# Adding the seven Strassen products up in PSUM banks, in the projections of a hybrid attention encoder layer

## The chip, the cores and the metric

The kernel runs as one program on one core of a Trainium2 chip. A core has a matrix engine (TensorE, "PE" in the profile, its weight loads "PEld"), a vector engine (VectorE, "DVE"), a scalar engine (ScalarE, "ACT"), a general engine (GpSimd, "POOL") and a queue that issues the transfers (SyncE, "SP"). The metric is the device time of one execution in microseconds; of several runs the median counts.

## What is computed

One encoder layer with d = 1024 over two batches that share the weights: a prompt of 512 tokens and a sample of 1024 tokens, all in float32. Cut to what matters here:

```python
def encoder_layer(x, ...):
    h = rms_norm(x, g_norm)
    u = h @ w_in                      # 1024 x 9728
    qa, ka, va, za, qb, kb, vb, zb, qc, kc, vc, zc, gl = jnp.split(u, offs, axis=-1)
    ya = neighborhood_attention(...)  # mixer A
    yb = diff_attention(...)          # mixer B
    yc = dilated_attention(...)       # mixer C
    pa = (ya * jax.nn.silu(za)) @ w_br_a
    ...
    merged = gates[:, :, 0] * pa + gates[:, :, 1] * pb + gates[:, :, 2] * pc
    return x + merged @ w_out
y = rms_norm(encoder_layer(x_prompt, ...), g_final)   # and the same of x_sample
```

## The kernel before

**Products.** `h @ w_in` and `merged @ w_out` are multiplied by Strassen's scheme in Winograd's form. A step takes two tiles of 128 columns of the weights (a *pair*), both halves of the 1024 rows, and both halves of the tokens: 256 tokens a half in the prompt, 512 in the sample. Instead of eight products of a quarter it makes seven, of sums of the weights (`s1` to `s4`, tiles `ws`) with sums of the tokens (`t1` to `t4`, made once by `sums`). Each product is twelve matmuls into one PSUM bank (`mm3`): the weights' rounded part `wh`, their remainder `wl`, and `wh` or a bfloat16 copy `wb` against the tokens' remainder. So a product needs a cast (`wh`), a subtraction (`wl <- x - wh`) and often a second cast (`wb`) before it, on ScalarE, VectorE or GpSimd. The tokens' operands are the tiles `tp` (prompt, and `tpb`, `tpl` for remainders), `th` and `tl` (sample). `strassen` does this for pairs and, at the end, for the output projection; `strassen_v` does it for three groups of four column tiles whose result is wanted with tokens on the partitions (weights' tiles `wq`).

**Adding up.** The seven products go to PSUM tiles named `p`, of which there are two (`PSUM_TAGS`). The first is copied to an SBUF tile `c`; each of the others is added to or from a `c` by VectorE, seven times in all, with the order that the formulas give: `c00`, then `c01` from `c00`, `c10` from `c01`, `c11` from `c10`. In the output projection the last addition goes to the residual tile `xt` straight from PSUM (`early`).

**Order.** All instructions are recorded first. `Program.order` then plays them through a model of the engines: an instruction that is ready and has a slot for its tiles is taken by the engine that is free, the oldest first, and that order is emitted. A copy or a cast may go to ScalarE or VectorE (`copy`, "AD"), a sum without PSUM to VectorE or GpSimd, and `better` gives it to the engine that the model thinks is done first. The engines of `wl` are fixed by a table (`LE`), those of `ws` are GpSimd (`SE`). The eight PSUM banks are one class `b` with a cap for each tag:

```python
RESERVE = {'e': 2, 's': 0, 'p': 2}
...
PSUM_TAGS = {'p': 2, 's': 3, 't': 2, 'o': 1}
for _t, _n in PSUM_TAGS.items():
    CAPS[_t] = ("b", _n)
```

Here `s` is scores, `t` transposes, `o` attention outputs. Every emitted instruction has the same source line (L418), so rows are told apart by tiles.

**Stages.** The prompt's 38 steps come first. The sample's 38 steps follow, with the attention units of both batches spread between them. Then the branches are merged (`merge`), and the output projection runs in six calls of `output`.

Of the kernel before, what the change touches and what calls it, by code (L numbers as in the profile page):

```python
# [18 lines left out]
D = 1024  # L19
# [49 lines left out]
class Buf:  # L69
    """A logical tile: one of the slots of its tag holds it from its first to its last instruction."""  # L70

    def __init__(self, prog, tag, shape, dtype, name):
        self.prog, self.tag, self.shape, self.dtype, self.name = prog, tag, list(shape), dtype, name
        self.free = int(np.prod(shape[1:]))
        self.seq = self.slot = self.real = None
        self.left = 0
        self.acc, self.last = [], []
# [68 lines left out]
class Program:  # L146
    """Records instructions, orders them by a model of the engines, and emits them in that order."""
# [92 lines left out]
    def price(self, eng, meth, args, kw):  # L240
        """Microseconds that an instruction holds its engine, those to its result, and those of the DMA rings."""
# [179 lines left out]
# the scheduler: latency between engines, instructions looked ahead, slots of a tag that stay free for older tiles  # L421
# [3 lines left out]
# engines of the sums of weights (P: GpSimd, D: VectorE), of the low parts of weights for the seven products of a pair  # L425
# (prompt, sample beside mixer B, sample beside the others), and query tiles whose two maps GpSimd joins in mixer B
# [4 lines left out]
# where the sample's operands are made, pairs multiplied directly, slots of the column quads, and the attention units:  # L431
# their starts in slots of the sample's stream and their order
# [8 lines left out]
# slots of each size, and for each tag its size and how many it may hold  # L441
# [14 lines left out]
PSUM_TAGS = {'p': 2, 's': 3, 't': 2, 'o': 1}  # L456
# [4 lines left out]
def build(ctx, tc, a):  # L461
# [18 lines left out]
    def copy(dst, src, scale=None, engines="AD"):  # L480
        """dst <- scale * src, on the engine that is done first."""
# [12 lines left out]
    def split(hi, lo, x, scale=None, psum=False, lo_on="DP"):  # L494
        """hi <- round(scale * x), lo <- scale * x - hi, both float32r."""
# [19 lines left out]
    def preamble():  # L515
# [15 lines left out]
        # padded relative position bias, masked outside each query column's window  # L531
# [31 lines left out]
    def put(dst, src, t, lo_on="DP"):  # L563
        """Columns 128 t .. of an operand (hi, lo) <- src."""
# [8 lines left out]
    def sums(T, t, f):  # L573
        """The operands of T that are sums, of the quarters in f, which is overwritten."""
# [8 lines left out]
        tt(f10, f11, f10, OP.subtract)  # L583
# [78 lines left out]
    def split_w(raw, lo_on="DP", half=True):  # L662
        """hi and lo of [128, n, 128] weights, and their bfloat16 or once more hi."""
# [10 lines left out]
    def mm3(ps, w, xh, xl):  # L674
        """ps <- the sum of w[k]^T (xh[k] + xl[k]) over k."""
        n = len(xh)
        for k in range(n):
            pe.matmul(ps, w[0][k], xh[k], start=k == 0, stop=False)
        for k in range(n):
            pe.matmul(ps, w[1][k], xh[k], start=False, stop=False)  # L680
        for k in range(n):
            pe.matmul(ps, w[2][k], xl[k], start=False, stop=k == n - 1)

    def strassen(raw, T, n, put, direct=False, early=None):
        """raw^T times the matrix of T: put(i, j, tile) for tile i of the 256 columns of raw and half j of T's."""
# [19 lines left out]
        def mul(x, q, on):  # L705
            hi, lo = T[q]
            w = split_w(x, on, q not in ("t1", "t2", "t3"))
            ps = pg.tile("p", [128, 512], F32)[:, :n]
            mm3(ps, w, [hi[:, k] for k in range(4)],
                [lo[k // 2][:, k % 2] if isinstance(lo, list) else lo[:, k] for k in range(4)])  # L710
# [24 lines left out]
        c01 = out(0, 1)  # L735
# [5 lines left out]
        p = mul(a1, "b10", LX[2])  # L741
        tt(c00, p, c00, OP.add, "D")
        done(0, 0, c00)
        c10 = out(1, 0)
        yield
        p = mul(s3, "t3", LX[3])
        tt(c10, p, c01, OP.add, "D")
        c11 = out(1, 1)
# [6 lines left out]
        p = mul(b1, "t4", LX[5])  # L755
        tt(c10, c10, p, OP.subtract, "D")
        done(1, 0, c10)
        yield
        if early:
            early(0, 1, c01)  # L760
            done(0, 1, mul(s4, "b11", LX[6]))
        else:
            p = mul(s4, "b11", LX[6])
            tt(c01, p, c01, OP.add, "D")
            done(0, 1, c01)
# [817 lines left out]
```

## Time and profile before

| | |
|---|---|
| runs | 2077.75, 2090.3, 2093.19 us, median 2090.3 |
| span of the profiled execution | 2095.2 us |
| TensorE | busy 1957.3 us, 93%, granted clock 0.979 on the mean |
| VectorE | busy 1733.3 us, 83% |
| ScalarE | busy 1053.0 us, 50% |
| GpSimd | busy 1108.8 us, 53% |
| DMA | 287.20 MB, 137 GB/s |

The profile is of one execution, whose span runs from its first to its last instruction; no other time of that execution is shown. Busy is not the same as working: TensorE's matmuls overlap, and an instruction of VectorE or GpSimd that is held up after its start counts as busy.

### The profile page before, as it was taken

The numbers are of one execution on the slowest core, as the hardware profiler recorded it, in microseconds if no ns is written. First come the engines' busy times: TensorE is split into PE (matmuls) and PEld (weight loads), VectorE is DVE, ScalarE is ACT, GpSimd is POOL, SyncE is SP. The second block draws the span as 40 slices with busy tenths as digits, with TensorE's granted clock in tenths as the row PEclk, the third lists the DMA queues.
The fourth block names the chain that finished last, engine by engine and source line by source line (L and its number), as shares of the span: only waits on it lengthen the run. The fifth ranks groups of instructions, "written<-read, shape, count | busy, mean of one in ns | idle before, by whom it ended". The sixth has DMA issues, their size and how long they took to land. (4 is left out here: it accounts for less than half of the span.)

```text
span 2095.2 us, 33259 instructions
## 1 busy us (share of the span) xinstructions
PE 1957.3 (93%) x11436; PEld 1490.6 (71%) x11436; DVE 1733.3 (83%) x3029; ACT 1053.0 (50%) x2052; POOL 1108.8 (53%) x788
## 2 busy tenths in 40 slices
PE   6998988788999999999999999999999999999998
PEld 6988877777877766666766677776765666666675
DVE  8999999999888577787888898566578777999698
ACT  5554455554455453254555546456546656544243
POOL 4897786767445344445454353632554333432485
PEclk9999999999999999999999999998999999999999
DMA  5554433435233435352213132333445455876642
GB/s 170 158 176 137 147 110 117 139 124 170 71 117 101 142 115 183 99 168 75 86 66 102 56 100 101 116 112 119 126 128 169 119 146 176 278 261 224 239 150 91
DMA packets 242343, 287.20 MB, mean 137 GB/s; under 512 B 33182, under 2 KB 168574, under 8 KB 242174
## 3 DMA queue, kind: packets, MB, share of 16 engines
q1 hardware_dynamic: 242174, 285.08, 42.6%
q8 instruction: 90, 1.47, 0.3%
q14 instruction: 79, 0.65, 0.1%
HBM read 203.93 MB, written 81.44 MB: 136 GB/s over the span
## 5 line engine op out<-in xcount | busy, mean ns | idle before, releaser
L418 PE MATMUL p<-th,wh 128*128 128x512 f32 x1400 | 435.4, 424 | 2.6 <-ACT wh L418 2.3
L418 DVE TENSOR_TENSOR c<-p,c 128x512 f32<-128x512 f32 (+1 forms) x462 | 260.2, 576 | 160.4 <-PE p L418 143.3
L418 POOL TENSOR_TENSOR wl<-ws,wh 128x512 fp32r<-128x512 f32 x143 | 202.9, 1419 | 263.7 <-ACT wh L418 133.6
L418 POOL TENSOR_TENSOR wl<-raw,wh 128x512 fp32r<-128x512 f32 (+1 forms) x159 | 228.8, 1439 | 185.2 <-PE o L418 42.5
L418 POOL TENSOR_TENSOR ws<-raw 128x512 f32<-128x512 f32 x156 | 233.2, 1496 | 147.6 <-DMA raw<-w_in 60.3
L418 PEld LDWEIGHTS p<-th,wh 128*128 128x128 f32 x1400 | 251.5, 191 | 75.1 <-issue 21.0
L418 PE MATMUL p<-th,wl 128*128 128x512 f32 x1016 | 297.8, 404 | 0.5 <-DVE wl L418 0.4
L418 ACT ACTIVATE wb<-raw 128x512 bf16<-128x512 f32 (+1 forms) x232 | 141.9, 612 | 235.9 <-PE p L418 134.5
L418 PE MATMUL s<-qk 128*128 128x512 f32 (+5 forms) x736 | 228.7, 422 | 7.3 <-DVE qk L418 5.3
L418 PEld LDWEIGHTS p<-th,wl 128*128 128x128 f32 x1016 | 188.7, 191 | 43.7 <-issue 5.6
L418 PEld LDWEIGHTS <-wb 128*128 128x128 bf16 x1376 | 107.0, 98 | 109.9 <-issue 54.1
L418 PE MATMUL p<-tp,wl 128*128 128x256 f32 x892 | 153.0, 294 | 34.3 <-DVE wl L418 32.7
L418 PEld LDWEIGHTS s<-qk 128*128 128x128 f32 (+1 forms) x736 | 117.0, 190 | 92.3 <-issue 61.3
L418 ACT ACTIVATE pt<-t 128x512 fp32r<-128x512 f32 (+4 forms) x173 | 90.4, 542 | 161.8 <-PE t L418 148.7
L418 PE MATMUL p<-tl,wb 128*128 128x512 bf16 x608 | 167.1, 384 | 0.0
L418 PE MATMUL p<-tp,wh 128*128 128x256 f32 x892 | 156.4, 298 | 8.1 <-DVE wh L418 7.1
L418 PEld LDWEIGHTS p<-tp,wl 128*128 128x128 f32 x892 | 124.0, 194 | 47.7 <-DVE wl L418 45.1
L418 ACT ACTIVATE e<-e,st 128x384 f32<-128x384 f32 (+2 forms) x192 | 105.5, 551 | 103.1 <-DVE st L418 101.8
L418 DVE TENSOR_TENSOR wl<-ws,wh 128x512 fp32r<-128x512 f32 x133 | 152.2, 1146 | 1.5
L418 DVE CUSTOM_DVE_ANT_0 e<-s,tab 128x384 f32<-128x384 f32 (+3 forms) x256 | 129.2, 531 | 28.8 <-PE s L418 23.1
L418 ACT ACTIVATE wh<-raw 128x512 fp32r<-128x512 f32 (+1 forms) x211 | 127.4, 604 | 41.5 <-PE p L418 9.7
L418 PE MATMUL t<-ident,e 128*128 128x128 f32 x672 | 123.6, 281 | 16.0 <-DVE e L418 14.4
(235 smaller groups left out, 4230.3 us busy)
## 6 DMA issues: line engine op xcount, KB each, us to landing
raw<-w_in SPq DMA_DIRECT2D x140, 512.0 KB
Us<-c SPq DMA_DIRECT2D x128, 256.0 KB
Up<-c SPq DMA_DIRECT2D x64, 256.0 KB
stg<-Us SPq DMA_DIRECT2D x30, 512.0 KB
g<-Us SPq DMA_DIRECT2D x48, 256.0 KB
tab<-E SPq DMA_DIRECT2D x192, 48.0 KB
stp<-Up SPq DMA_DIRECT2D x30, 256.0 KB
YG<-y SPq DMA_DIRECT2D x30, 256.0 KB
```

Of the source, the lines that this page charges most:

```text
L418: getattr(engs[o.eng], o.meth)(*[val(x) for x in o.args], **{k: val(x) for k, x in o.kw.items()})
```

## The change

`strassen` and `strassen_v` open one bank `A` with the first product (`a0 b00`), copy it out, add the next product into the same bank, copy that out, and so on. Four results leave that bank as copies: `c00`'s part, `c01`'s part, `c11`'s part and `c10`. Two other banks serve the rest: `B` takes `a1 b10`, which is added to `c00`; `C` takes `s1 t1`, which is added to `c11`, and then `s4 b11` on top of it, which is added to `c01`. To make all signs positive, the sum `t4` of the tokens is taken the other way round. The order of the products is a0 b00, a1 b10, s2 t2, s1 t1, s3 t3, b1 t4, s4 b11. `p` may have four banks instead of two, the caps of the other tags stay. In the output projection `early` takes the two copies `c00` and `c01` to the residual at once, and three results go to it straight from PSUM. `strassen_v` makes four sums of weights instead of five. The engines' tables and the model's prices are the same.

```diff
-PSUM_TAGS = {'p': 2, 's': 3, 't': 2, 'o': 1}
+PSUM_TAGS = {'p': 4, 's': 3, 't': 2, 'o': 1}
...
             if kw["start"]:
                 preds.update(o for p0, p1, o in b.last if p0 < box[1] and box[0] < p1)
+                b.opened = [x for x in b.opened if x[0] >= box[1] or box[0] >= x[1]] + [(box[0], box[1], op)]
+            else:
+                preds.update(o for p0, p1, o in b.opened if p0 < box[1] and box[0] < p1)
...
-        tt(f10, f11, f10, OP.subtract)
+        tt(f10, f10, f11, OP.subtract)
...
-    def mm3(ps, w, xh, xl):
+    def mm3(ps, w, xh, xl, first=True):
...
-            pe.matmul(ps, w[0][k], xh[k], start=k == 0, stop=False)
+            pe.matmul(ps, w[0][k], xh[k], start=first and k == 0, stop=False, **kw)
...
+        def part(i, j, ps):
+
+            c = out(i, j)
+            copy(c, ps)
+            if early and i + j < 2:
+                early(i, j, c)
+            return c
+
+        def rest(i, j, c, ps):
+
+            if early and i + j < 2:
+                done(i, j, ps)
+            else:
+                tt(c, ps, c, OP.add, "D")
+                done(i, j, c)
...
-        c00 = out(0, 0)
-        p = mul(a0, "b00", LX[0])
-        copy(c00, p)
+        A = mul(a0, "b00", LX[0])
+        c00 = part(0, 0, A)
+        yield
+        B = mul(a1, "b10", LX[2])
+        rest(0, 0, c00, B)
...
-        p = mul(s2, "t2", LX[1])
-        tt(c01, p, c00, OP.add, "D")
+        mul(s2, "t2", LX[1], A)
+        c01 = part(0, 1, A)
...
-        p = mul(s1, "t1", LX[4])
-        tt(c11, p, c10, OP.add, "D")
-        done(1, 1, c11)
-        tt(c01, p, c01, OP.add, "D")
+        C = mul(s1, "t1", LX[4])
+        yield
+        mul(s3, "t3", LX[3], A)
+        c11 = part(1, 1, A)
+        rest(1, 1, c11, C)
...
+        mul(b1, "t4", LX[5], A)
...
+            c10 = out(1, 0)
+            copy(c10, A)
+            done(1, 0, c10)
+        yield
+        mul(s4, "b11", LX[6], C)
+        rest(0, 1, c01, C)
```

What it does to the order is seen in one pair of the prompt, the last before the first group of four. First TensorE's queue, in the kernel before. `tp_722`, `tp_734` and `tp_793` are t3, t1 and t4; each product has a bank of its own name (`p_2795`, `p_2812`, `p_2837`):

```order
L418 MATMUL p_2795<-tp_722,wh_2752 128x256 [waits Activation_49]
L418 MATMUL p_2795<-tp_722,wh_2752 128x256 x3
L418 MATMUL p_2795<-tp_722,wl_2766 128x256 [waits DVE_49]
L418 MATMUL p_2795<-tp_722,wl_2766 128x256 x3
L418 MATMUL p_2795<-tpb_760,wh_2752 128x256 x2
L418 MATMUL p_2795<-tpb_766,wh_2752 128x256 x2
L418 MATMUL p_2812<-tp_734,wh_2775 128x256 [waits Activation_49]
L418 MATMUL p_2812<-tp_734,wh_2775 128x256 x3
L418 MATMUL p_2812<-tp_734,wl_2791 128x256 [waits DVE_49]
L418 MATMUL p_2812<-tp_734,wl_2791 128x256 x3
L418 MATMUL p_2812<-tpl_748,wh_2775 128x256 x4
L418 MATMUL p_2837<-tp_793,wh_2785 128x256 [waits Activation_49]
```

The same place of the changed kernel, one pair earlier, where `p_2487` is bank A (`tp_724` is t3, `tp_795` t4), `p_2569` bank C and `p_2635` the next pair's A:

```order
L421 MATMUL p_2569<-tpl_755,wh_2542 128x256 x4
L421 MATMUL p_2487<-tp_724,wh_2564 128x256 [waits Activation_49]
L421 MATMUL p_2487<-tp_724,wh_2564 128x256 x3
L421 MATMUL p_2487<-tp_724,wl_2594 128x256 [waits DVE_49]
L421 MATMUL p_2487<-tp_724,wl_2594 128x256 x3
L421 MATMUL p_2487<-tpb_728,wh_2564 128x256 x2
L421 MATMUL p_2487<-tpb_768,wh_2564 128x256 x2
L421 MATMUL p_2635<-tp_578,wh_2629 128x256 [waits DVE_49]
L421 MATMUL p_2635<-tp_578,wh_2629 128x256
L421 MATMUL p_2487<-tp_795,wh_2603 128x256 [waits Activation_49]
L421 MATMUL p_2487<-tp_795,wh_2603 128x256 x3
```

The products t3 and t4 now stand in one bank with two matmuls of the next pair between them, and the wait for ScalarE at t4's first matmul is for the copy that empties the bank.

Then VectorE's queue, of before:

```order
L418 TENSOR_TENSOR c_2769<-p_2741,c_2769 128x256 [waits PE_49,Activation_49,Pool_49]
L418 TENSOR_TENSOR wl_2791<-ws_2637,wh_2775 128x512 [waits DVE_49,PE_49,Activation_49]
L418 TENSOR_TENSOR c_2769<-p_2773,c_2769 128x256 [waits DVE_49,PE_49]
L418 TENSOR_TENSOR c_2822<-p_2795,c_2769 128x256 [waits DVE_49,PE_49]
L418 CAST wq_2829<-rawq_2458 128x512 [waits DMAHW6_49]
L418 TENSOR_TENSOR wl_2834<-ws_2737,wh_2814 128x512 [waits Activation_49]
L418 TENSOR_TENSOR c_2822<-p_2812,c_2822 128x256 [waits DVE_49,PE_49]
L418 TENSOR_TENSOR c_2769<-p_2812,c_2769 128x256
```

and of the changed kernel:

```order
L421 TENSOR_TENSOR c_2572<-p_2530,c_2572 128x256 [waits PE_49,Activation_49]
L421 TENSOR_TENSOR wl_2594<-ws_2500,wh_2564 128x512
L421 CAST wh_2603<-raw_2240 128x512 [waits DMAHW4_49]
L421 CAST wh_2609<-ws_2539 128x512 [waits PE_49]
L421 TENSOR_TENSOR wl_2622<-ws_2539,wh_2609 128x512 [waits DVE_49,PE_49]
L421 CAST wh_2629<-raw_2328 128x512 [waits DMAHW2_49,PE_49]
L421 TENSOR_TENSOR c_2633<-p_2569,c_2633 128x256 [waits DMAHW6_49,Activation_49]
L421 CAST wh_2644<-raw_2387 128x512 [waits PE_49]
L421 TENSOR_TENSOR wl_2669<-raw_2387,wh_2644 128x512 [waits DVE_49,PE_49,Pool_49]
L421 TENSOR_TENSOR c_2572<-p_2569,c_2572 128x256 [waits PE_49]
```

Fewer additions out of PSUM stand there, and the casts `wh` that ScalarE did have moved in between. Counted over the whole order, VectorE has 318 additions out of PSUM fewer, 150 casts `wh` and 45 copies out of `p` more (3029 instructions become 2961); ScalarE has 183 copies out of `p` more and 150 casts `wh` fewer (1727 become 1717); GpSimd has 18 fewer (788 become 770). The matmuls and the transfers are the same in number.

## Rows read from the trace of the kernel before

**Rows 1.** The page: busy time, share and instructions of an engine.

```profile
PE 1957.3 (93%) x11436; PEld 1490.6 (71%) x11436; DVE 1733.3 (83%) x3029; ACT 1053.0 (50%) x2052; POOL 1108.8 (53%) x788
```

**Rows 2.** Busy time by stage: stretch, length; PE, PEld, DVE, ACT, POOL; clock, DMA.

```profile
0.00:530.00 530.00, 456.29 (x3511) 420.25 (x3512) 497.64 (x679) 275.20 (x508) 389.07 (x265) 0.98 0.46 145
530.00:1750.00 1220.00, 1171.90 (x6425) 846.07 (x6424) 937.64 (x1910) 632.73 (x1233) 558.26 (x401) 0.98 0.36 114
1960.00:2095.20 135.20, 125.64 (x550) 90.32 (x548) 114.12 (x137) 51.92 (x113) 97.65 (x72) 0.98 0.40 147
```

**Rows 3.** Waits of PE, 0 to 530 us: us in total, times, longest.

```profile
PE p L418 <- DVE wl L418: 32.7, 42, 1.9
PE p L418 <- DVE wq L418: 16.3, 18, 2.1
PE t L418 <- DVE xp L418: 14.9, 4, 8.4
PE p L418 <- DVE wh L418: 7.1, 8, 2.2
```

**Rows 4.** Waits of PE, 530 to 1800 us, first and fifth.

```profile
PE t L418 <- DVE e L418: 14.4, 15, 2.3
...
PE o L418 <- DVE pt L418: 5.1, 4, 3.8
```

**Rows 5.** Timeline of VectorE, 299.9 to 309.2 us: start, length, instruction.

```profile
300.40 1.50 DVE L418 CAST wq<-ws 128x512 fp32r<-128x512 f32 x1
...
304.13 1.76 DVE L418 TENSOR_TENSOR wq<-ws,wq 128x512 fp32r<-128x512 f32 x1
...
308.22 0.68 DVE L418 TENSOR_TENSOR wq<-ws,wq 128x512 fp32r<-128x512 f32 x1
308.82 0.41 DVE L418 CAST wq<-rawq 128x512 fp32r<-128x512 f32 x1
```

**Rows 6.** Timeline of GpSimd in that stretch, and one instruction at 2081 us.

```profile
299.89 3.16 POOL L418 TENSOR_TENSOR ws<-rawq 128x512 f32<-128x512 f32 x2
303.83 1.50 POOL L418 TENSOR_TENSOR wl<-raw,wh 128x512 fp32r<-128x512 f32 x1 [0.78 <-ACT wq L418]
...
2081.38 1.28 POOL L418 TENSOR_TENSOR wl<-ws,wh 128x512 fp32r<-128x512 f32 x1 [3.24 <-ACT wh L418]
```

**Rows 7.** Groups of VectorE, 0 to 530 us: count, busy us, mean ns, idle before.

```profile
L418 DVE TENSOR_TENSOR c<-p,c 128x256 f32<-128x256 f32 x186 | 73.6, 413 | 10.6 <-PE p L418 10.3
L418 DVE CAST wh<-ws 128x512 fp32r<-128x512 f32 x39 | 38.8, 994 | 2.1 <-POOL ws L418 2.0
...
L418 DVE CAST wh<-raw 128x512 fp32r<-128x512 f32 x5 | 4.1, 822 | 0.0
```

**Rows 8.** Groups of VectorE and ScalarE, whole span.

```profile
L418 DVE TENSOR_TENSOR c<-p,c 128x512 f32<-128x512 f32 x276 | 186.6, 686 | 149.9 <-PE p L418 133.0 <-issue 6.3 <-ACT ft L418 3.7
L418 DVE CAST wh<-ws 128x512 fp32r<-128x512 f32 x82 | 65.4, 798 | 2.1 <-POOL ws L418 2.0
L418 DVE CAST wh<-raw 128x512 fp32r<-128x512 f32 x47 | 34.6, 737 | 0.0
...
L418 ACT ACTIVATE c<-p 128x512 f32<-128x512 f32 x39 | 22.9, 587 | 21.4 <-PE p L418 20.5 <-ACT qk L418 0.8
...
L418 ACT ACTIVATE c<-p 128x256 f32<-128x256 f32 x34 | 12.7, 374 | 7.3 <-PE p L418 5.7 <-POOL ws L418 1.6
```

**Rows 9.** Timeline around one copy out of PSUM, 61 to 85 us.

```profile
60.94 0.61 PE L418 MATMUL p<-tpb,wb 128*128 128x256 bf16 x4
...
61.65 0.39 ACT L418 ACTIVATE c<-p 128x256 f32<-128x256 f32 x1 [0.83 <-PE p L418]
...
82.09 1.66 DVE L418 TENSOR_TENSOR wl<-ws,wh 128x512 fp32r<-128x512 f32 x1
...
83.80 0.74 PE L418 MATMUL p<-tp,wl 128*128 128x256 f32 x4
```

**Rows 10.** Waits of all engines: who waited for whom, us in total, times, longest.

```profile
ACT e L418 <- DVE st L418: 101.8, 67, 8.2
```

More of the change, by code (lines that the diff above doesn't have):

```diff
@@ L76, in __init__ @@
         self.left = 0
-        self.acc, self.last = [], []
+        self.acc, self.last, self.opened = [], [], []
 class View:
@@ L672, in split_w @@
         return [[w[:, k] for k in range(n)] for w in ws]
[L674 removed]
+    def mm3(ps, w, xh, xl, first=True):
         n = len(xh)
+        kw = {} if first else {"skip_group_check": True}
         for k in range(n):
[L678 removed]
+            pe.matmul(ps, w[0][k], xh[k], start=first and k == 0, stop=False, **kw)
         for k in range(n):
[L680 removed]
+            pe.matmul(ps, w[1][k], xh[k], start=False, stop=False, **kw)
         for k in range(n):
[L682 removed]
+            pe.matmul(ps, w[2][k], xl[k], start=False, stop=k == n - 1, **kw)
     def strassen(raw, T, n, put, direct=False, early=None):
@@ L703, in ws, with mul @@
             return s
-        def mul(x, q, on):
+        def mul(x, q, on, ps=None):
             hi, lo = T[q]
             w = split_w(x, on, q not in ("t1", "t2", "t3"))
-            ps = pg.tile("p", [128, 512], F32)[:, :n]
+            first = ps is None
+            if first:
+                ps = pg.tile("p", [128, 512], F32)[:, :n]
             mm3(ps, w, [hi[:, k] for k in range(4)],
-                [lo[k // 2][:, k % 2] if isinstance(lo, list) else lo[:, k] for k in range(4)])
+                [lo[k // 2][:, k % 2] if isinstance(lo, list) else lo[:, k] for k in range(4)], first)
             return ps
@@ L781, in ws, with mul @@
             return dst
-        def mul(x, q, on):
+        def mul(x, q, on, ps=None):
             hi, lo = T[q]
-            ps = [pg.tile("p", [128, 2, 256], F32) for _ in pairs]
+            first = ps is None
+            if first:
+                ps = [pg.tile("p", [128, 2, 256], F32) for _ in pairs]
             w = [[], [], []]
@@ L807, in mul @@
                         z = lo[:, k]
-                    pe.matmul(ps[c // 2][:, c % 2], z[:, s], w[i % 6 // 2][k // 2][:, k % 2], start=i == 0, stop=i == 11)
-            return ps
-        def out():
-            return [pg.tile("c", [128, 2, 256], F32) for _ in pairs]
+                    pe.matmul(ps[c // 2][:, c % 2], z[:, s], w[i % 6 // 2][k // 2][:, k % 2],
+                              start=first and i == 0 and c % 2 == 0, stop=i == 11,
+                              skip_group_check=True)
+            return ps
         def done(i, j, c):
@@ L816, in done, with part, rest @@
                 put(i, j, k, c[k])
[L818 removed]
+        def part(ps):
+            c = [pg.tile("c", [128, 2, 256], F32) for _ in pairs]
             for k in pairs:
[L820 to L826 removed]
+                copy(c[k], ps[k])
+            return c
+        def rest(i, j, c, ps):
+            for k in pairs:
+                tt(c[k], ps[k], c[k], OP.add, "D")
+            done(i, j, c)
+        s1 = ws(b0, b1, OP.add)
+        A = mul(a0, "b00", LE['p'][0])
+        c00 = part(A)
         yield
         yield
[L829 to L832 removed]
+        s2 = ws(s1, a0, OP.subtract)
+        B = mul(a1, "b10", LE['p'][2])
+        rest(0, 0, c00, B)
         yield
         yield
[L835 removed]
+        mul(s2, "t2", LE['p'][1], A)
+        c01 = part(A)
         ws(a1, s2, OP.subtract, s2)
[L837 to L838 removed]
         yield
         yield
[L841 to L844 removed]
+        C = mul(s1, "t1", LE['p'][4])
+        ws(a0, b0, OP.subtract, s1)
         yield
         yield
[L847 to L851 removed]
+        mul(s1, "t3", LE['p'][3], A)
+        c11 = part(A)
+        rest(1, 1, c11, C)
         yield
         yield
[L854 to L856 removed]
+        mul(b1, "t4", LE['p'][5], A)
+        done(1, 0, part(A))
         yield
         yield
[L859 to L861 removed]
+        mul(s2, "b11", LE['p'][6], C)
+        rest(0, 1, c01, C)
         yield
```

52 lines of the change are left out of this document (3 added, 49 removed).

## Prediction

> **What bounds the kernel now.** I read first who is busy, then the same by stage, then who waits for whom. Over the span TensorE is busy 93% and VectorE 83% [rows 1], but the average mixes two different programs [rows 2]. From 530 to 1750 us, the sample, TensorE is busy 1171.9 of 1220 us and VectorE 77%: TensorE sets the pace. What TensorE waits for there is thirteen small items of VectorE and ScalarE, from 14.4 us down to 0.3 us (the first and the fifth are shown), 48 us in all [rows 4]. In the first 530 us, the prompt, it is the other way round: VectorE is busy 497.6 us (94%), TensorE 456.3 us, and TensorE's waits, 71 us in four rows, are all for VectorE, and for the two-input subtractions and casts of weights (`wl`, `wq`, `wh`) above all, never for an addition out of PSUM [rows 3].
>
> Why VectorE is full there is seen at 300 us. A cast of 512 columns takes 1.50 us while GpSimd is at work, and 0.41 us after it has stopped; a subtraction of two SBUF tiles takes 1.76 us and 0.68 us in the same way [rows 5, 6]. GpSimd's sums take 1.28 us where they start first, 1.5 us and more otherwise [rows 6]. An addition out of PSUM shows nothing of this: 186 of them average 413 ns [rows 7], and I take them to run beside GpSimd. So in the prompt the two engines take turns at something that they share. Counted with the durations alone, the stretch has 246 sums and subtractions of 512 columns on GpSimd (of its 265 instructions), 262 two-input instructions and 94 casts on VectorE (of its 679): 246 x 1.28 + 262 x 0.68 + 94 x 0.41 = 315 + 178 + 39 = 532 us, in a stretch of 530. That sum is an upper estimate, since the ends of instructions may overlap, but it says that turns alone can fill the prompt.
>
> **The change part by part.** *Additions.* 318 additions out of PSUM leave VectorE. What stands in their place is seen in the order: most copies go to ScalarE, and 150 casts `wh` have moved from ScalarE to VectorE, as the model levels the two. Over the whole span VectorE loses 194 x 0.686 + 124 x 0.413 = 184 us and gains 101 casts at 0.737 and 49 at 0.798 = 114 us and 45 copies at no more than an addition's 0.686 = 31 us [rows 7, 8]: -39 us of 1733. ScalarE has 183 copies for 150 casts, which is about even. The relief is small, and what counts is where it falls.
>
> *Prompt, VectorE.* There 124 additions of 256 columns and 12 of 512 go: -51.2 - 8.2 = -59 us. Net 61 casts come (`wh` of plain weights from 5 to 74, a few others fewer), and 5 copies at 0.41 = 2 us. A cast of that kind averaged 822 ns in five samples, and 994 ns for weights' sums [rows 7]; at 0.82 it is +50 us, so -7 us. The ends are -32 us (each cast alone, 0.41) and +35 us (each beside GpSimd, 1.50).
>
> *Prompt, turns.* The additions that go took no turns; the 61 casts that come do. 61 x 0.41 = +25 us, less 8 sums fewer on GpSimd, -10 us: +15 us on the sum of 532. Since that sum equals the whole stretch, I weigh it above VectorE's own -7 and take **+8 us**, ends -32 and +35.
>
> The Trainium skill has a rule that speaks against this change (SBUF — State Buffer, Who interferes with whom): the ports that VectorE and GpSimd share are an exclusive lock, taken by casts, copies and two-input operations from SBUF, while an instruction with at most one SBUF input outside the fast modes does not contend. By it the additions out of PSUM were free for GpSimd and the casts are not; the rows of 0.41 and 1.50 us agree [rows 5]. By it the prompt's term would be the turns' +15; with no lock it would be VectorE's -7.
>
> *Bank A.* A product now may not start in A before the last one has been copied out. From the rows: the last matmul of a product is over 0.28 us after its start (four take 0.61 us at 0.11 us each [rows 9]), the copy starts up to 0.1 us later and takes 0.374 us at 256 columns (0.587 at 512, [rows 8]), and a matmul follows its releaser by 0.05 us (82.09 + 1.66 to 83.80 [rows 9]). That is about 0.75 us from the start of the last matmul, and about 1.07 us at 512 columns (a copy 0.21 us longer, a matmul of twice the width). The order gives 95 such waits in the prompt, 80 in the sample and 13 in the output projection; the order of before has none this short, since two banks took turns. At some 0.12 us a matmul (0.23 at 512 columns), 42 of the 95 have less than 0.75 us of other matmuls between, and the shortages add up to 10 us in the prompt, 3 in the sample, 1.6 in the output, if ScalarE copies at once. If it comes 0.4 us late, they are 28, 7 and 4 us; 0.6 us late, 38, 11 and 5 us. In the prompt TensorE already waits 71 us for VectorE, and most of a shortage lies inside those waits: I take **+3** there, **+3** in the sample, where nothing covers it, and **+1** in the output. Behind the waiting matmul all of TensorE's queue stands, since it is in order, and the additions of B and C on VectorE wait for it.
>
> *Sample, waits for VectorE.* VectorE stood 133 us waiting for products before an addition of 512 columns [rows 8], with softmax work queued behind it. There are 182 such additions fewer after the prompt, and 40 copies more. Of the 48 us that TensorE waits there for others I take **-3 us** back, ends 0 and -20. ScalarE now holds more copies that wait for TensorE and has the same softmax work queued; it waited 101.8 us for VectorE's maxima, once for 8.2 us [rows 10].
>
> *Nothing:* four banks for `p` (scores, transposes and outputs share the other four; their places relative to the products hardly move in the order); t4 with the other sign; the smaller number of sums on GpSimd after the prompt, where it is 46% busy [rows 2]; the end of the output projection, which still closes on the product s4 b11 and one operation from PSUM. If the cover of TensorE's 96% in the sample went, these would show first as waits for `s` and `t` tiles.
>
> **Sum:** +8 +3 +3 +1 -3 = **+12 us**. The profiled span is 2095.2 us, 0.2% above the median of the three runs, 2090.3 us; on the median that gives **2102 us**, 0.6% slower, which I count as no change: the three runs lie 0.7% apart, so about 1% is what a measurement of this kernel can tell.
>
> **The rivals.**
>
> *Late copies (slower).* The chain through A is four copies long, and ScalarE is in order: a copy behind a cast that waits for a slot, or behind an `exp` that waits for VectorE, comes late, and each time the whole of TensorE stands. From a mean lateness of 0.4 us on, it decides. At 0.6 us, with nothing hidden: 38 + 11 + 5 = 54, with +8 and -3: 2090 + 59 = 2149 us. For it: ScalarE's waits for VectorE [rows 10] and places in the order with two or three matmuls between a product in A and the next. Against it: ScalarE is busy 52% in both stages, and the prompt's waits are covered.
>
> *Every cast at the price beside GpSimd (slower).* 61 casts at 1.50 us: +35 instead of +8, so 2090 + 35 + 4 = 2129 us. For it: 1.50 us stands in the rows [rows 5]. Against it: the 39 casts of weights' sums averaged 994 ns [rows 7]. The lock that the Trainium skill states (SBUF — State Buffer, Who interferes with whom) would make this of it where neither engine ever rests.
>
> *VectorE was the bound and is relieved (faster).* If its own time sets the prompt and the casts mostly run alone: -32; if the additions blocked the softmax work: -20; the chain +7: 2090 - 45 = 2045 us. For it: 94% in the prompt, all of TensorE's waits there for VectorE [rows 2, 3]. Against it: the relief is filled with casts, in the very stage that it should help.
>
> **How the numbers follow.** The forecast, within 1% (2069 to 2111): 0.44. Late copies: 0.20. Casts beside GpSimd: 0.16. Relief: 0.20. So faster by over 1%: 0.20; within 1%: 0.44; slower by over 1%: 0.36. The range leaves out the better half of the relief and the worse half of the late copies, 0.10 each: 2058 to 2140 us.
>
> **What the changed kernel's profile would show.** VectorE still busy over 90% in the prompt, the additions of 256 columns halved, and a group of some 70 casts `wh<-raw` there at 0.7 to 1.0 us; a mean under 0.5 speaks for relief, over 1.2 for the second rival. TensorE's waits for a `c` of ScalarE, none before, at 5 to 20 us in total; over 40 us is the first rival. TensorE's waits for `wl` and `wq` in the prompt about as before; if they fall under 30 us in total, the turns were not the bound. The sample stretch should keep its length within 10 us. I am wrong if TensorE's time without waits changes at all, for the matmuls are the same.

## The result, and the profile after

The changed kernel takes 2158.93 us (median of four runs, 2153.81 to 2162.56) against 2091.62 us of the kernel before in the same comparison: ratio 1.0333 [1.0302, 1.0365], 3.3% slower. The forecast was 2102 us, and the time lies outside its range of 2058 to 2140.

The profiled span is 2160.0 us, 64.8 us longer than that of before. First the page, the rows that answer to [rows 1]:

```profile
span 2160.0 us, 32897 instructions
PE 1979.8 (92%) x11353; PEld 1511.2 (70%) x11436; DVE 1713.6 (79%) x2961; ACT 1024.4 (47%) x2042; POOL 1077.0 (50%) x770
```

VectorE is busy 20 us less, ScalarE 29 us less, GpSimd 32 us less, in a longer span: all three stand idle more. The stages of [rows 2] say where:

```profile
0.00:530.00 530.00, 437.06 (x3300) 405.43 (x3301) 466.24 (x580) 262.82 (x528) 353.28 (x247) 0.95 0.44 136
530.00:1750.00 1220.00, 1153.96 (x6281) 840.97 (x6337) 904.15 (x1853) 590.48 (x1153) 538.34 (x386) 0.97 0.36 112
```

In the first 530 us TensorE got through 3300 matmuls where it had got through 3511, VectorE fell from 94% to 88%, and the granted clock from 0.98 to 0.95. The stages' ends are read from TensorE's timeline: the prompt's last matmul, and the first matmul of the merge. Before:

```profile
502.00 0.61 PE L418 MATMUL p<-tpb,wb 128*128 128x256 bf16 x4
...
1798.03 0.72 PE L418 MATMUL s<-ych,wh 128*128 128x512 f32 x2
```

After:

```profile
535.01 0.61 PE L421 MATMUL p<-tpb,wb 128*128 128x256 bf16 x4
...
1858.87 0.71 PE L421 MATMUL s<-ych,wh 128*128 128x512 f32 x2
```

So the prompt is 33.0 us longer (502.6 to 535.6), the sample 27.8 us (1295.4 to 1323.2), and what follows 4 us. Cut at these ends, the prompt and the sample of the kernel before:

```profile
0.00:502.61 502.61, 430.41 (x3302) 396.08 (x3303) 474.18 (x652) 264.94 (x491) 373.29 (x255) 0.98 0.46 144
502.61:1798.03 1295.42, 1244.68 (x6907) 902.70 (x6906) 999.16 (x2027) 670.77 (x1316) 591.64 (x424) 0.98 0.38 118
```

and of the changed one:

```profile
0.00:535.62 535.62, 439.60 (x3321) 407.52 (x3321) 471.79 (x586) 263.45 (x529) 357.99 (x249) 0.95 0.44 137
535.62:1858.87 1323.25, 1255.84 (x6821) 910.90 (x6881) 986.60 (x2027) 643.55 (x1269) 579.65 (x414) 0.97 0.37 114
```

Of the prompt's 33.0 us, 23.8 are time in which TensorE is idle and 9.2 are busy time; of the sample's 27.8 us, 16.7 are idle and 11.2 busy. Some matmuls of the sample stand before the prompt's last one, 2 in the kernel before and 21 in the changed one (3 us of work).

TensorE's waits in the first 530 us, which answer to [rows 3]:

```profile
PE p L421 <- DVE wh L421: 36.0, 23, 2.9
PE t L421 <- DVE xp L421: 14.9, 4, 8.5
PE p L421 <- DVE c L421: 11.8, 7, 4.4
PE p L421 <- DVE wl L421: 9.5, 10, 1.7
PE p L421 <- DVE wq L421: 8.3, 8, 1.5
PE p L421 <- ACT c L421: 4.4, 3, 3.4
```

The remainders `wl` and `wq`, 49.0 us before, have fallen to 17.8; the copies out of a bank, which did not exist as a releaser, cost 16.2; and the cast `wh` on VectorE went from 7.1 to 36.0, in 23 waits of about 1.5 us each. All waits of this stretch together rose from 72.6 to 92.5 us. The 9.2 us of busy time are the sample's early matmuls and the clock: the lower level of 1.2 GHz holds in about 54 us of the prompt (twice 0.05 of 535.6) against 20 to 25 before, and a run of four matmuls that takes 0.61 us at the upper level takes 1.08 us there. By these figures the 30 us more would be worth about 13 at most, an estimate; the busy time shows less.

The groups of VectorE in the first 530 us, as in [rows 7]:

```profile
L421 DVE CAST wh<-raw 128x512 fp32r<-128x512 f32 x74 | 74.1, 1001 | 0.1
...
L421 DVE TENSOR_TENSOR c<-p,c 128x256 f32<-128x256 f32 x91 | 38.0, 418 | 25.9 <-PE p L421 19.7 <-ACT c L421 6.0
...
L421 DVE CAST wh<-ws 128x512 fp32r<-128x512 f32 x29 | 22.8, 785 | 3.7 <-PE p L421 3.2
```

The casts came in the number forecast (74) and at 1.00 us. What they do to TensorE is seen in the timeline of one pair. VectorE:

```profile
107.22 0.41 DVE L421 CAST wh<-raw 128x512 fp32r<-128x512 f32 x1
107.72 0.43 DVE L421 CAST wh<-ws 128x512 fp32r<-128x512 f32 x1
108.31 1.76 DVE L421 TENSOR_TENSOR wl<-ws,wh 128x512 fp32r<-128x512 f32 x1 [0.17 <-PE p L421]
110.00 1.49 DVE L421 CAST wh<-raw 128x512 fp32r<-128x512 f32 x1
```

TensorE and ScalarE beside it:

```profile
109.68 0.64 PE L421 MATMUL p<-tpb,wh 128*128 128x256 f32 x4
111.54 0.98 PE L421 MATMUL p<-tp,wh 128*128 128x256 f32 x6 [1.22 <-DVE wh L421]
...
108.19 0.38 ACT L421 ACTIVATE c<-p 128x256 f32<-128x256 f32 x1 [1.42 <-PE p L421]
110.36 0.38 ACT L421 ACTIVATE c<-p 128x256 f32<-128x256 f32 x1 [1.78 <-PE p L421]
```

TensorE has ended the product t3 at 110.3 us and stands until the cast that began at 110.00 has ended. It is the cast of the *next* pair's first product, `a0 b00`: in the order shown with the change, `wh_2629` right behind `wl_2622`, the remainder for this pair's last product. TensorE is not out of work. The six matmuls at 111.54 are the two of the next pair that the order puts between t3 and t4, and the first four of t4 behind them. The weights of t4 were cast at 107.22 and its bank was copied out at 110.74, so by these rows t4 could have begun about 0.8 us before the two did, had they not stood in front of it. They fill the time in which ScalarE copies bank A. Of the 23 pairs of the prompt whose first cast is on VectorE, 21 have two or four matmuls ahead of t4 of the pair before; in the order of before, where t4 has a bank of its own, no pair has any. And 21 of the 23 waits, 32.9 of the 36.0 us, are for a `wh<-raw` right behind a subtraction.

The scheduler's model holds the two for 0.60 and 0.33 us (512 x 0.00104 + 0.068 and 512 x 0.00052 + 0.068); here, with GpSimd at work, they take 1.76 and 1.49. ScalarE, which does these casts in 0.62 us and did all 31 of them in the prompt of before, idles before each of its two copies out of the bank, waiting for TensorE. In the changed order 23 of the prompt's 31 first casts are on VectorE.

The Trainium skill (SBUF — State Buffer, Who interferes with whom) has casts from SBUF, in VectorE's fast modes, and operations with two SBUF inputs take ports that VectorE shares with GpSimd, and an addition with its one SBUF input leave them alone. The trace agrees: a cast of the same shape takes 0.43 us at 107.72, where GpSimd stands idle, and 1.49 us two rows on, where it works, and the additions take 418 ns on the mean.

### The profile page after: what moved, and what is told of

It reads as the page before. It is cut to its first block, busy times and chain, and to the rows that moved or that the text cites. A ratio compares the mean times of both kernels' runs of the same rounds, so it can differ in the third digit from the quotient of the medians.

```text
span 2160.0 us, 32897 instructions
## 1 busy us (share of the span) xinstructions
PE 1979.8 (92%) x11353; PEld 1511.2 (70%) x11436; DVE 1713.6 (79%) x2961; ACT 1024.4 (47%) x2042; POOL 1077.0 (50%) x770
## 5 line engine op out<-in xcount | busy, mean ns | idle before, releaser
L421 PE MATMUL p<-th,wh 128*128 128x512 f32 x1400 | 441.7, 427 | 13.2 <-DVE wh L421 7.3
L421 POOL TENSOR_TENSOR wl<-raw,wh 128x512 fp32r<-128x512 f32 x155 | 226.3, 1460 | 247.4 <-DVE wh L421 49.5
L421 POOL TENSOR_TENSOR ws<-raw 128x512 f32<-128x512 f32 x150 | 215.2, 1436 | 262.0 <-DMA raw<-w_in 98.9
L421 ACT ACTIVATE c<-p 128x512 f32<-128x512 f32 (+1 forms) x256 | 125.1, 489 | 253.6 <-PE p L421 238.3
L421 ACT ACTIVATE wb<-raw 128x512 bf16<-128x512 f32 (+1 forms) x221 | 134.6, 610 | 210.2 <-PE p L421 143.9
L421 DVE TENSOR_TENSOR c<-p,c 128x512 f32<-128x512 f32 (+1 forms) x222 | 127.3, 574 | 106.1 <-PE p L421 78.6
L421 PEld LDWEIGHTS p<-tp,wh 128*128 128x128 f32 x892 | 127.6, 202 | 66.7 <-DVE wh L421 41.1
L421 ACT ACTIVATE pt<-t 128x384 f32<-128x384 f32 (+4 forms) x158 | 82.5, 537 | 164.9 <-PE t L421 155.4
L421 PE MATMUL p<-tl,wb 128*128 128x512 bf16 x539 | 148.9, 382 | 4.6 <-issue 0.6
L421 PEld LDWEIGHTS p<-tp,wl 128*128 128x128 f32 x892 | 129.6, 200 | 16.2 <-DVE wl L421 12.0
L421 PE MATMUL p<-wq,th 128*128 128x256 f32 x816 | 132.3, 299 | 5.0 <-DVE wq L421 3.4
```

Source lines behind the costliest of these rows:

```text
L421: getattr(engs[o.eng], o.meth)(*[val(x) for x in o.args], **{k: val(x) for k, x in o.kw.items()})
```

## The experiments

Kernels of one comparison share its runs of the kernel before. The table has each run's ratio, the length of the prompt and of the sample, read as above, and TensorE's waits in the first 530 us for VectorE's `wh`, for its `wl` and `wq`, and for the copies `c` of either engine (us). Each length is from one profile. In the kernels with the chain 14 to 33 matmuls of the sample (2 to 5 us of work) stand before the prompt's last one, in the others one or two, so a difference of under 5 us in a stage between a kernel with the chain and one without says little.

| kernel | median | ratio | prompt | sample | wh | wl, wq | c |
|---|---|---|---|---|---|---|---|
| before | 2091.62 | | 502.6 | 1295.4 | 7.1 | 49.0 | 0 |
| changed | 2158.93 | 1.0333 [1.0302, 1.0365] | 535.6 | 1323.2 | 36.0 | 17.8 | 16.2 |
| e1 fresh banks | 2106.44 | 1.0100 [1.0069, 1.0130] | 507.0 | 1303.4 | 4.8 | 51.2 | 0 |
| e2 casts on ScalarE | 2279.77 | 1.0925 [1.0900, 1.0950] | 581.8 | 1363.3 | 0 | 28.8 | 56.0 |
| e3 copies on VectorE | 2102.42 | 1.0077 [1.0055, 1.0099] | 504.9 | 1290.3 | 0 | 7.2 | 40.4 |
| e4 four banks alone | 2098.37 | 1.0068 [1.0043, 1.0093] | 510.1 | 1298.6 | 8.7 | 44.2 | 0 |
| e5 true length | 2099.64 | 1.0035 [1.0013, 1.0057] | 509.9 | 1292.3 | 1.1 | 18.5 | 25.0 |
| e17 the same, of before | 2086.58 | 0.9984 [0.9968, 0.9999] | 499.6 | 1296.7 | 5.3 | 35.9 | 0 |
| e10c engines kept | 2153.07 | 1.0302 [1.0276, 1.0328] | 542.2 | 1311.1 | 36.9 | 25.6 | 14.7 |
| e10 kept, true length | 2107.31 | 1.0089 [1.0068, 1.0110] | 523.2 | 1293.4 | 2.4 | 16.5 | 36.3 |
| e12 latency 0.45 | 2154.39 | 1.0320 [1.0299, 1.0340] | 540.8 | 1313.0 | 40.1 | 16.3 | 14.1 |
| e13 latency 0.43 | 2161.95 | 1.0359 [1.0332, 1.0386] | 534.2 | 1326.8 | 33.9 | 21.7 | 11.4 |
| e8 c11's copy on VectorE | 2102.56 | 1.0062 [1.0040, 1.0085] | 517.2 | 1284.4 | 0.8 | 28.8 | 26.9 |
| e15 first casts on ScalarE | 2131.79 | 1.0201 [1.0175, 1.0227] | 511.3 | 1316.9 | 1.6 | 26.4 | 17.1 |
| e16c engines kept, before | 2120.28 | 1.0155 [1.0116, 1.0193] | 507.4 | 1318.3 | 7.9 | 50.0 | 0 |
| e16 first casts on VectorE, before | 2132.26 | 1.0203 [1.0176, 1.0230] | 520.5 | 1311.1 | 11.4 | 52.4 | 0 |
| e7 true price | 2063.01 | 0.9862 [0.9824, 0.9900] | 497.0 | 1269.2 | 0 | 14.7 | 30.5 |
| e7b the same, of before | 2062.00 | 0.9862 [0.9821, 0.9903] | 485.8 | 1281.8 | 3.6 | 34.1 | 0 |
| e18 true prices, two | 2042.62 | 0.9776 [0.9747, 0.9806] | 485.9 | 1255.1 | 0 | 19.6 | 5.3 |
| e18b the same, of before | 2050.80 | 0.9823 [0.9789, 0.9857] | 481.9 | 1280.3 | 0 | 23.7 | 0 |

### The parts alone

**e1**, the changed kernel without the chain: each product opens a bank of its own, so that the results hold fewer products than they should.

```diff
-            first = ps is None
-            if first:
-                ps = pg.tile("p", [128, 512], F32)[:, :n]
+            first = True
+            ps = pg.tile("p", [128, 512], F32)[:, :n]
...
-        mul(s2, "t2", LX[1], A)
+        A = mul(s2, "t2", LX[1], A)
```

> The changed kernel, but every product starts in a bank of its own (the products of A and C are not added up, so the results are not the sums; that part of the computation is left out). Copies, additions, casts and their engines stay nearly as in the changed kernel (265 instead of 280 casts wh on VectorE). Theory CHAIN (the loss is TensorE waiting until bank A has been copied out): about 2095 us, the waits of p for a c gone. Theory CASTS (the loss is the casts wh that the model moved into VectorE's queue, where they come late): about 2150 us, with the waits of p for wh on VectorE at some 40 us as before.

+1.0%, with 265 casts `wh` on VectorE (280 in the changed kernel). The moved casts without the chain cost a third of the loss, and TensorE's waits are those of before. This run says more than it was made for. In 20 pairs of the prompt the first cast is on VectorE, right behind a subtraction, as in the changed kernel; yet TensorE waits 4.8 us for `wh` in all, for none of these casts, and the prompt is 4.4 us longer, not 33.0. What is missing is the bank to wait for: no matmul of the next pair stands ahead of t4 in any pair. So the place on VectorE costs TensorE no wait by itself.

**e2**, `split_w` lets only ScalarE make `wh` (`copy(hi, x, scale, "A")`).

> The changed kernel with the casts wh of pairs on ScalarE alone; copies out of p and casts wb then go to VectorE (262 copies there). Bank A is chained as in the changed kernel. CASTS: about 2105 us, p's waits for wh on VectorE gone. CHAIN: about 2150 us or more, since the copies now stand in VectorE's fuller queue; p's waits for a c of VectorE rise to over 30 us.

+9.3%: the balance then put the copies out of `p`, 262 of them, and most casts to bfloat16 on VectorE, and TensorE waited 55.3 us for VectorE's copies alone. It tells nothing on the casts, only what a fixed engine does to everything that is left free.

**e3**, copies out of `p` on VectorE (`copy(c, ps, engines="D")` in three places).

> The changed kernel with all copies out of p on VectorE: 306 copies and 222 additions there, and the casts go back to ScalarE (163 wh on VectorE against 130 in the kernel before and 280 in the changed one). CASTS: about 2105 us. CHAIN: 2150 us or more, with p waiting for a c of VectorE over 40 us in the prompt.

+0.8%. The chain is whole, and its waits are seen in full:

```profile
PE p L421 <- DVE c L421: 40.4, 40, 4.4
PE t L421 <- DVE xp L421: 16.5, 4, 9.2
PE p L421 <- ACT wh L421: 5.4, 7, 2.2
PE p L421 <- DVE wl L421: 5.3, 8, 1.8
```

40 us of them take the place of the 49 us for remainders, and the prompt is 2.3 us longer than before. Here the chain's waits are covered nearly in full, as forecast.

**e4**, the kernel before with `PSUM_TAGS = {'p': 4, ...}`.

> The kernel before with four banks allowed for p instead of two, nothing else. If banks taken from scores, transposes and outputs are part of the loss (theory BANKS): 2105 to 2125 us, the extra in the sample stretch. If not: 2085 to 2097 us.

+0.7%, between the two ranges: two more banks for the old sums are no gain. The extra is in the prompt (7.5 us), not in the sample, where the theory of the banks had it.

### The length that the plan believes

**e5**, the changed kernel, in `Program.order` after an instruction has been chosen:

```diff
+                    if e == "DVE" and pick.meth == "tensor_copy" and pick.args[1].buf.tag not in PSUM_TAGS:
+                        pick.cost += 0.00092 * pick.args[0].size()
```

> The changed kernel, whose plan lets a cast or copy from SBUF hold VectorE for 0.92 ns more per element (0.47 us more at 512 columns, about what the trace shows beside GpSimd) once its engine has been chosen; choice and price tables stay. The plan then gives VectorE 213 casts wh (280 in the changed kernel). Theory of the plan (VectorE's casts last two to three times what the plan holds, so that a bank chain without slack gets its weights late): most of the loss goes, to about 2110 us, ratio under 1.015, and TensorE's waits in the first 530 us for wh of VectorE fall from 36 to under 12 us. Theory of the hop (a copy by ScalarE, then an addition by VectorE, with the casts queued behind it): the hops stay, 2135 to 2155 us, and VectorE's waits for a c of ScalarE stay over 15 us of the 22.8.

3.0 of the 3.3% are gone, and of the 36.0 us for `wh` 1.1 are left. VectorE's waits for ScalarE's `c`, which the theory of the hop blamed, grew over the whole span from

```profile
DVE c L421 <- ACT c L421: 22.8, 21, 6.5
```

in the changed kernel to

```profile
DVE c L423 <- ACT c L423: 32.2, 25, 6.7
```

here. The theory of the hop falls.

**e17**, the same two lines in the kernel before.

> The kernel before with a plan that lets VectorE's casts and copies from SBUF last 0.92 ns more per element, prices of the choice as they were: the control of the run that took 3.0% from the changed kernel. VectorE has 121 casts wh in place of 130. If the wrong length costs the chain only: within 0.7%, 2075 to 2105 us. If a truer plan helps any kernel as much: 2030 us.

-0.2%: the old sums did not suffer from the wrong length.

**e10c** and **e10**. In e5 the casts on VectorE became fewer too (213). So all 2233 choices of an engine were taken from the changed kernel's order as a list; e10 has e5's two lines beside it, e10c has not.

```diff
+        several = [o for o in self.ops if len(o.ways) > 1]
+        for o, e in zip(several, FIXED, strict=True):
+            o.ways = [w for w in o.ways if w[0][0] == e]
```

> The same list of engines, the plan with the old prices: the control of the run before, since to fix the engines changes some places in the order. Theory of the plan: 2140 to 2165 us, at least 1.5% above its twin with the true plan. Theory of the share: 2140 to 2165 us, like its twin. Theory of the draw: anywhere from 2090 to 2160 us, and no order between the two.

> The changed kernel with every instruction on the engine that it has there (280 casts wh on VectorE, 256 copies on ScalarE), written down as a list, and a plan that lets VectorE's casts and copies from SBUF last 0.92 ns more per element. Theory of the plan: the same work in an order that knows the true length of the casts gives most of the loss back, 2090 to 2115 us. Theory of the share (too many casts on VectorE and copies on ScalarE, whatever the order): 2140 to 2165 us. Theory of the draw (the order of the changed kernel is an unlucky one of many that lie a per cent or two apart): 2100 to 2130 us, and its twin with the old prices the same within 1%.

1.030 against 1.009: the same instructions on the same engines, in another order, 46 us apart, 19.0 of them in the prompt and 17.7 in the sample. The order shows what moved at the place of above. VectorE's queue in e10, where `raw_2330` is the next pair's first half:

```order
201 L427 CAST wh_2609<-ws_2539 128x512
202 L427 CAST wh_2625<-raw_2330 128x512
203 L427 TENSOR_TENSOR wl_2631<-ws_2539,wh_2609 128x512
```

The next pair's cast now stands ahead of the remainder. That is so in 11 of the 23 pairs; and in 22 of the 23 no matmul of the next pair stands ahead of t4 any more. The timeline of VectorE in e10, at that stage of a pair:

```profile
102.95 1.51 DVE L427 CAST wh<-ws 128x512 fp32r<-128x512 f32 x1
104.38 1.50 DVE L427 CAST wh<-raw 128x512 fp32r<-128x512 f32 x1
105.80 1.78 DVE L427 TENSOR_TENSOR wl<-ws,wh 128x512 fp32r<-128x512 f32 x1
```

The cast and the subtraction are as long as ever, and TensorE's waits for `wh` are 2.4 us in all. What it waits for is the chain, at 36.3 us:

```profile
PE p L427 <- DVE c L427: 18.4, 20, 3.9
PE p L427 <- ACT c L427: 17.9, 27, 4.1
```

It is not all covered: the prompt of e10 is still 20.6 us longer than before, that of e5 7.3.

**e12** and **e13**, the changed kernel with `LAT = 0.45` and `LAT = 0.43` in place of 0.44, a reshuffle without a reason behind it.

> The changed kernel with the model's latency between engines at 0.45 in place of 0.44 us: a reshuffle of the order without a reason behind it (VectorE has 274 casts wh, ScalarE 258 copies). Theory of the plan and theory of the share: the cause is still there, 2140 to 2170 us. Theory of the draw: well below, 2090 to 2135 us.

> The same with 0.43 us (277 casts wh on VectorE, 265 copies on ScalarE). Theory of the plan and theory of the share: 2140 to 2170 us. Theory of the draw: 2090 to 2135 us.

1.032 and 1.036, with 40.1 and 33.9 us for `wh`. The loss is no accident of one order: in both, 20 and more pairs of the prompt have matmuls of the next pair ahead of t4 that need a cast of VectorE.

### The place

**e8**, the copy of c11's part on VectorE (`copy(c, ps, engines="D" if i + j == 2 else "A")`), the other copies on ScalarE.

> The changed kernel with one of the four copies of a pair, the one of c11's part, which is followed at once by an addition on VectorE, put on VectorE, and the others on ScalarE: no hop from ScalarE to VectorE there. VectorE keeps 262 casts wh. Theory of the hop: most of the loss goes, 2105 to 2120 us, and VectorE's waits for a c of ScalarE fall from 22.8 to under 6 us. Theory of the plan: the casts are late as before, 2145 us or more, and TensorE's waits for wh of VectorE in the first 530 us stay over 25 us.

1.006, as the theory of the hop had it. But here the balance gave all 31 first casts of the prompt back to ScalarE (and in e3 likewise), though VectorE keeps 262 casts `wh`: the two kernels with the chain and the old plan that lack the loss are those without a first cast on VectorE in the prompt. This led to the next pair.

**e15**, e10c's list with 45 letters changed: first casts go to ScalarE, all 23 of the prompt that VectorE had and 22 after it. Counted in the order, the 22 are 17 of the sample's 23 and 5 of the output projection; 6 of the sample's stay on VectorE.

> The changed kernel with every instruction on its own engine, as a list, and the old prices in the plan, but for 45 casts: the cast wh of a pair's first product (a0 b00), which the changed kernel has on VectorE in 23 pairs of the prompt and 22 of the sample, goes to ScalarE. The twin without this is at 1.030. Theory of the one place (the 36 us for wh are 22 waits of about 1.5 us, one a pair, for this cast behind a subtraction on VectorE, and they are most of the loss): the waits for wh of VectorE in the first 530 us fall under 5 us and the time to 2095 to 2115 us, ratio 1.003 to 1.012. Theory of the whole plan (any late cast takes its place as the next bound): 2130 us or more.

The prompt falls by 30.9 us (542.2 to 511.3) and the waits for `wh` from 36.9 to 1.6 us: in the prompt it is that place. In 27 of 30 pairs three or four matmuls of the next pair now stand ahead of t4, and with ScalarE's cast in time they do no harm. In all, though, only 1.0% comes back, since the sample stays long (1316.9). The expectation of 1.003 to 1.012 failed there.

**e16c** and **e16**, the same list for the kernel before, without and with 41 of those casts on VectorE (23 in the prompt, 13 in the sample, 5 in the output projection).

> The kernel before with its engines as a list and nothing else: the control of the run with the first products' casts on VectorE (1.020). If that run's 2% are those 41 casts: within 0.7% of the kernel before, 2075 to 2105 us. If it is the list that costs: 2115 us or more.

> The kernel before with its engines as a list, but for the same casts of a0 b00, 41 of them, put on VectorE as in the changed kernel (23 of the prompt, 18 of the sample). If that place is costly by itself: 1.5 to 3% slower than the kernel before, 2120 us or more. If it is costly only where the products are chained through a bank, because two banks in turn let the next pair begin early: within 1%, 2080 to 2110 us.

The list by itself costs the kernel before 1.55%, 23 us of it in the sample, against what was expected, so e16 is read against e16c alone: 0.5% slower, with intervals that overlap, the prompt 13.1 us longer. The same casts cost the old sums less than half of the 30.9 us that they cost the chain, and little of it as waits for `wh`, which rose from 7.9 to 11.4 us: as in e1, no matmul of the next pair stands ahead of t4.

### The price

**e7**, the changed kernel with the model's price of a VectorE cast or copy from SBUF raised from 0.33 to 0.81 us at 512 columns, in the choice of engine too; **e7b**, the same in the kernel before.

```diff
-            return n * (0.00104 if psum or two else 0.00052) + 0.068 + 0.06 * ptr, LAT, 0
+            return n * (0.00104 if psum or two else 0.00144 if meth == "tensor_copy" else 0.00052) + 0.068 + 0.06 * ptr, LAT, 0
```

> The changed kernel with the model's price of a cast or copy from SBUF on VectorE raised from 0.33 to 0.81 us at 512 columns, in the choice too: VectorE keeps 57 casts wh of 280, ScalarE does 478, and copies out of PSUM move in part to VectorE (89 of 311). Theory of the plan: 2095 to 2110 us, ratio 1.00 to 1.01, waits for wh of VectorE in the first 530 us under 8 us. Theory of the hop: 222 copies stay on ScalarE, which is fuller, so 2130 us or more.

> The kernel before with the same raised price (VectorE 53 casts wh instead of 130, ScalarE 482). Control: if the price is simply better for any kernel, it is faster than the kernel before, 2065 to 2080 us, and the gain of the raised price in the changed kernel counts for less; if the plan of before had slack enough for late casts (both theories), it is within 1%, 2075 to 2100 us.

Both are 1.4% faster than the kernel before, faster than any theory had it, and level with each other: the raised price is simply better, for either kernel.

**e18** and **e18b**, with the price of a two-input operation on SBUF tiles of 512 columns raised from 0.60 to 1.40 us as well.

```diff
+            ... 0.0026 if two and n == 512 else ...
```

> The changed kernel with the raised price of SBUF casts on VectorE (as in the run at 0.986) and the model's price of a two-input operation on two SBUF tiles of 512 columns raised from 0.60 to 1.40 us, between the 0.68 and 1.76 us of the trace. If VectorE's turns with GpSimd are still under-planned there: faster than 2063 us, 2030 to 2055. If the choice of engines is what counted: 2055 to 2075 us.

> The kernel before with the two raised prices of the run at 0.978. With the raised price of casts alone the two kernels were level, 2063 and 2062 us. If adding up in PSUM banks is worth something once the plan is true, since VectorE has 318 additions less: 2055 us or more, above the 2042.6 us of the changed kernel with both prices. If it is worth nothing: 2035 to 2050 us.

2042.62 us (2040.71 to 2045.09) is the fastest kernel of this study, 2.2% below the kernel before. e18b has 2050.80 (2044.71 to 2053.19), between its two ranges. The page of e18:

```profile
PE 1950.3 (96%) x11436; PEld 1489.6 (73%) x11436; DVE 1419.1 (70%) x2473; ACT 1257.0 (62%) x2465; POOL 1178.6 (58%) x835
```

and of e18b:

```profile
PE 1952.8 (95%) x11436; PEld 1493.2 (73%) x11436; DVE 1544.7 (75%) x2715; ACT 1194.9 (58%) x2306; POOL 1211.5 (59%) x848
```

With prices near the trace the change takes 126 us off VectorE, and nearly nothing off the time: the two ratios' intervals overlap, so a gain of 0.5% is not settled. In these single profiles the changed kernel loses in the prompt (+11.2 us in e7, +4.0 in e18, against the kernel before at the same prices) and gains in the sample (-12.6 and -25.2); in what follows the sample it loses again (+5.1 and +9.9). The +4.0 are within what the sample's early matmuls make of it.

## Why the prediction was wrong

**The step that failed in the prompt** is that "Prompt, turns", +8 us, and "Bank A", +3 us, were sized apart and added. The casts without the chain made the prompt 4.4 us longer (e1), the chain without first casts on VectorE 2.3 to 14.6 us (e3, e15, e8). Together they made it 33.0. "Bank A" counted the matmuls that stand between two products in A as cover for the copy, at their own length. In 21 pairs of the prompt that cover is the next pair's first matmuls, whose weights come from a cast that has moved to VectorE, and they wait themselves, with t4 behind them. "Prompt, turns" costed the casts as shares of a sum of busy times that happened to equal the stretch, and so as engine time. But the prompt is not filled by turns: with the casts there, VectorE has fallen to 88%, where over 90% were forecast, and the waits for `wl` and `wq` to 17.8 us, which the prediction had named as the sign that the turns are not the bound. The price of a late cast stood in the right row (1.50 us, [rows 5]); what was missing is its place. The order shown in the part on the change has the casts one behind the other and the two matmuls between t3 and t4; the prediction did not ask what waits behind each cast.

**A term put at nothing** is TensorE's own time: the prediction held it fixed, since the matmuls are the same, and named any change of it as a sign of being wrong. It rose from 1957.3 to 1979.8 us, 22 of the 64.8 us, with a mean granted clock of 0.968 against 0.979.

**The step that failed in the sample** is the sum of +3 for the chain and -3 for relief; +27.8 us were measured, of which 16.7 are idle time of TensorE and 11.2 busy time. TensorE's waits between 530 and 1800 us, a window that leaves out the last 59 us of the changed kernel's sample, are 64.1 us against 48.3, in 21 items of which the largest are:

```profile
PE t L421 <- DVE tab L421: 12.1, 7, 3.9
PE s L421 <- DVE qk L421: 7.5, 5, 2.6
PE p L421 <- DVE wh L421: 6.7, 5, 2.6
```

With the true length of casts in the plan they are 37.9 us (e10, against 61.1 in e10c), so a part may be the same wrong plan. But no one place was found, e15 moved 17 of the sample's 23 first casts and left it as long, and the list alone lengthens the sample of the kernel before by 23 us, more than the 17.7 us that lie between e10c and e10. How much of these 27.8 us is the change's and how much the order's stays open.

**Right**: the direct waits of the chain through bank A. TensorE's waits for ScalarE's copies are 7.7 us over the whole span (5 to 20 were forecast), 4.4 of them in the prompt, where VectorE's copies cost 11.8 more; late copies, the rival whose time of 2149 us came nearest, were not the mechanism. That the chain is covered holds for e3; in e15 and e8, without first casts on VectorE as well, the prompt is 8.7 and 14.6 us longer than before. So where +3 us fits, it is in part luck. Right too in the number and the price of the casts and in the small relief of VectorE (-20 us, -39 forecast). The second rival, casts at the price beside GpSimd, had the price and the sign; it made 2129 us of it, as engine time, where the chip made it a wait of TensorE.

**Shown and argued.** Shown: for the prompt, that neither the casts (e1, e16) nor the chain (e3, e8, e15) costs most of it alone, that the two do together, and that another order of the same instructions on the same engines takes the waits for `wh` away (e10 against e10c). Shown for the whole: with the engines kept, the order from true lengths is 2.1% faster, and three orders from the old prices (e10c, e12, e13) are as slow as the changed kernel. With the chain and no first cast on VectorE in the prompt the change is within 1% where the balance is made anew (e3, e8), and 2.0% slower where the other engines are kept (e15). Not shown: that the sample's part of the loss has the same cause; a draw of the order can be as large there. Only argued: why the model put the first casts on VectorE. It levels by its prices, and with ScalarE given 183 copies a cast at 0.33 us on VectorE looked nearer than one at 0.52 on ScalarE (512 x 0.000833 + 0.094); at 0.81 all 31 of the prompt went back to ScalarE (e7), which fits.

## What to carry to other kernels

Where a scheduler plays a model, a change that shifts the balance of its engines is judged by the model's prices: compare them with the trace first, above all for operations whose length depends on what another engine does. A moved instruction costs by its place: look at what is queued behind the first matmul that needs it, not at the sum of busy times. Work that fills a gap in an engine's queue is cover only if its own operands are there in time. Two parts of a change that are cheap alone can be dear together, so size them together where one feeds what covers the other. And before a change is blamed or praised, give the old kernel the same corrected prices; here that was worth 1.4 to 1.8%, the change itself nothing that is settled.

## What was not expected of the hardware

A partial sum can be copied out of a PSUM bank between two groups of matmuls at little cost: in e10 TensorE waits 17.9 us in 27 waits for ScalarE's copies, 0.66 us each. The Trainium skill (PSUM — Partial Sum Buffer, The four PSUM rules) says that the hardware allows a synchronised read of a partial sum in the middle of a group; the trace agrees and gives the price.

The order alone, with every engine fixed and no price changed, moved the kernel before by 1.55%; what it did to the changed one, 0.3%, is within the intervals.
